# A streaming encoder step: softmax maps combined out of PSUM, group norms placed later, cache outputs placed in the last projection

## The chip, the core and the metric

The kernel runs on one core of one Trainium2 chip. The metric is device time in microseconds: the time of one execution, given as the median of the runs. Engines are called PE (TensorE), DVE (VectorE), ACT (ScalarE), POOL (GpSimd) and SP (SyncE, which here issues nearly all DMAs).

## What is computed

Two layers over 512 prompt tokens and 32 sample tokens, width 1024, all in float32. Layer 0 is RWKV-7 time mixing and is not touched. Layer 1, which the change edits, is differential attention with 12 heads of width 128, plus four memory heads, a SiLU gate, an output projection and a final norm:

```python
def diff_attention(q, k_all, v_all, q_pos, k_pos, lam):
    ...
    mask = k_pos[None, :] < (q_pos[:, None] // CHUNK + 1) * CHUNK
    def probs(qa, ka):
        s = jnp.einsum('bqhd,bkhd->bhqk', qa, ka).astype(jnp.float32) * DF_HD ** -0.5
        return jax.nn.softmax(jnp.where(mask, s, NEG_INF), axis=-1)
    attn = probs(q1, k1) - lam * probs(q2, k2)
    return jnp.einsum('bhqk,bkhd->bqhd', attn.astype(v_all.dtype), v_all)
...
    o = rmsnorm(o, subln) * (1.0 - lam_init)
    y_mem = mem_attention(qm, mk, mv)
    out = jnp.concatenate([o.reshape(B, T, MIX_W).astype(x.dtype), y_mem], axis=-1) * jax.nn.silu(gate)
    return x + out @ w_out, k, v
```

The keys and values of all heads are outputs too (the caches). The 32 sample tokens attend to 128 cached keys and to themselves. Since the result of each head is normed over its 128 values, a common factor per row can be applied late, if the norm's epsilon sees the scaled values.

## The kernel before, in words

Layer 1 is one long stream of projections (`stream`, line 1742). Each block of 128 output columns takes 48 matmul positions: two halves of 272 tokens, eight slices of the contraction, three products each (high and low parts of float32 numbers kept as `float32r`). The list `makes` in `diff_layer` (line 1777) holds 56 such blocks: values, keys and queries of each head, gates (`GATES1` says under which head), and query and gate of a memory head under the heads in `MEM1`. Everything else is a small step hung into this stream with `at(position, step)`. The position counts the matmuls since the stage's start, and `f` is the position at which the head's blocks begin. So the numbers at the top of the file (`TILES1`, `BACK1`, `SUMS1`, `NORM1`, `SAMPLE1`, `MEMAT1`, those with a 2 for the last heads) are distances in matmuls. While `self.ordered` is set, the wrapper `Queue` (line 111) ties each instruction of PE, DVE, ACT and SP to the one before it on its engine, so those four run in the order written; POOL isn't tied. Instructions issued after `self.ordered = False` are placed by the framework.

The steps of one head, in order:

- `values_turn`, `keys`, `keys_out`: DVE transposes of v and k, written by SP to a DRAM scratch `scr`, one pair per group of four heads (keys and values).
- `scores(t)` for four tiles of 128 queries (line 1872): PE makes two maps (`ps_s`, tag "c" of the pool `psc`, two banks), DVE masks them and takes the maxima (`peaks`, `snm`).
- `powers(t)`: ACT takes the exponentials of both maps into `pt` in SBUF, with row sums in `rs` (`srs` in the profile).
- `turned(t)`: DVE inverts both sums, multiplies the second with minus lambda, scales the second map (`TENSOR_SCALAR`) and adds the scaled first (`SCALAR_TENSOR_TENSOR`; `combine`, line 2107), then transposes 32x32 blocks into `pk`.
- `weights_out`, `weights_back`: SP writes `pk` to DRAM (`ptr`) and reads it back as `aT`, a full transposition, with the head's values `vt`.
- `weighted` (line 1923): PE multiplies `aT` and `vt` into `ps_o` (pool `psx`, one bank); DVE copies to `ot`, ACT sums squares into `ss`.

The last head transposes on PE instead (`turned_here`, `ps_aT`). Per group of four heads, the sample tokens have their own chain (`sample_scores` to `sample_rows`, tiles `ps_sc`, `ps_saT`, `ps_os`, `ps_osT`), and then `norms` (an inverse square root of nine small DVE instructions on `oss`), `scaled` (four DVE multiplications of `ot`) and `finished` (PE transposes into `ps_oT`, pool `psm`, two banks; DVE multiplies with the gate in `og`). `kv_out` (line 2029) copies a group's `scr` to the output caches: for groups 0 and 1 inside the stream, under the second head of the next group; for group 2 in the last projection, after the first half of its third output block.

The last projection (`w_out`, line 1238, with `consume` of `layer1`, line 1721) makes eight output blocks in two halves each, adds the residual and collects the squares of the final norm. The halves of the last block are followed at once by the final outputs.

Of the kernel before, what the change touches and what calls it, by code (L numbers as in the profile page):

```python
# [9 lines left out]
F32 = mybir.dt.float32  # L10
# [3 lines left out]
AF = mybir.ActivationFunctionType  # L14
# [30 lines left out]
BACK1, SUMS1, NORM1 = 96, 160, 182  # L45
BACK2, SUMS2, NORM2 = 50, 100, 40
SUMS3 = 22
OUT1 = 36
RKV = 4
# [72 lines left out]
class Trunk:  # L122
# [1538 lines left out]
    def layer1(self):  # L1661
# [17 lines left out]
        with ExitStack() as ctx:  # L1679
# [97 lines left out]
    def diff_layer(self, p, mp, mctx, pool_early, order, made):  # L1777
# [6 lines left out]
        def at(pos, fn):  # L1784
            ev.append((pos, len(ev), fn))

        def copied(x):
# [75 lines left out]

        def exps(S, nm):
            n = S[0].shape[1]
            rs = p.tile([P, 2], F32, tag="srs", name="srs", bufs=3)
            pt = p.tile([P, 2, 512], F32, tag="pt", name="pt", bufs=2)
            for m in range(2):
                self.ae.activation(pt[:, m, :n], S[m], AF.Exp, bias=nm[:, m : m + 1], accum_out=rs[:, m : m + 1])
            return pt, rs  # L1870

        def scores(st, t):
            n, c, S = (t + 1) * P, slice(t * P, t * P + P), []
            if t == 0:
                st["pk"] = pk = p.tile([P, 40, 32], F32, tag="pk", name="pk", bufs=PKB)
                st["aT"] = pk[:].rearrange("p (i b) c -> p i (b c)", b=4)
            for m in range(2):
                ps = self.psc.tile([P, 512], F32, tag="c", name="ps_s")
                for i, x in enumerate((st["kh"], self.kz[st["h"] % 2])):
# [5 lines left out]
        def powers(st, t):  # L1885
            st["pt", t] = exps(*st["pt", t])

        def mixed(pt, rs, n):
            self.ve.reciprocal(rs[:], rs[:])
            self.combine(pt, rs, n, nlam)  # L1890

        def joined(st, t):
            mixed(*st["pt", t], (t + 1) * P)

        def turned(st, t):
            n, b0 = (t + 1) * P, 2 * t * (t + 1)
            joined(st, t)
            pt, rs = st.pop(("pt", t))
            self.ve.transpose(st["pk"][:, b0 : b0 + 4 * (t + 1)].rearrange("p b c -> p (b c)"), pt[:, 0, :n])

        def turned_here(st, t):
            n, i0 = (t + 1) * P, t * (t + 1) // 2
            pt, rs = st.pop(("pt", t))
            ps = self.psm.tile([P, 512], F32, tag="m", name="ps_aT")
            for i in range(t + 1):
                self.te.transpose(ps[:, i * P : i * P + P], pt[:, 0, i * P : i * P + P], self.ident[:])
            self.ae.copy(st["aT"][:, i0 : i0 + t + 1, :], ps[:, :n].rearrange("p (i c) -> p i c", c=P))
# [15 lines left out]
        def weighted(st):  # L1923
# [11 lines left out]
            for t in range(4):  # L1935
                jk = p.tile([P, P], F32, tag="jk", name="jk", bufs=1)
                self.ae.activation(jk[:], ot[:, t, :], AF.Square, accum_out=G["ss"][:, 0, 4 * j + t : 4 * j + t + 1])

        def opened(G, hg):
            G["scr"] = [self.dp.tile([T, 4, P], F32, tag=f"scr{i}", name=f"scr{i}", bufs=2) for i in range(2)]  # L1940
            G["on"] = []
# [18 lines left out]
        def sample_scores(G):  # L1960
            ps = [self.psc.tile([P, 512], F32, tag="c", name="ps_sc") for _ in range(2)]
# [6 lines left out]
            G["sp"] = exps(*peaks([x[:, : P + TS] for x in ps]))  # L1968
            G["vs"] = vs = p.tile([P, 4, P], F32, tag="ck", name="vs")
            self.se.dma_start(vs[:TS], G["scr"][1][TP:])  # L1970

        def sample_mixed(G):
            mixed(*G["sp"], 160)

        def sample_turned(G):
            pt, rs = G.pop("sp")
            ps = self.psm.tile([P, 512], F32, tag="m", name="ps_saT")
            self.te.transpose(ps[:, :P], pt[:, 0, :P], self.ident[:])
            self.te.transpose(ps[:TS, P : 2 * P], pt[:, 0, P:160], self.ident[:])
            G["saT"] = aT = p.tile([P, 2 * P], F32, tag="aTs", name="aTs")  # L1980
# [3 lines left out]
        def sample_weighted(G):  # L1984
            aT = G["saT"]
            po = self.psx.tile([P, 512], F32, tag="x", name="ps_os")
            for j in range(4):
# [6 lines left out]
            G["os"] = os_ = p.tile([P, P], F32, tag="os", name="os")  # L1994
            G["s2"] = s2 = p.tile([P, 3], F32, tag="os2", name="os2")
            self.ve.tensor_copy(os_[:], po[:, :P])
            jk = p.tile([P, P], F32, tag="jk", name="jks", bufs=1)
            self.ae.activation(jk[:], os_[:], AF.Square, accum_out=s2[:, 0:1])

        def sample_norm(G):  # L2000
            os_, s2 = G["os"], G["s2"]
            self.ve.tensor_scalar(s2[:, 1:2], s2[:, 0:1], 1.0 / P, EPS, ALU.mult, ALU.add)
            self.rsqrt(s2[:, 2:3], s2[:, 1:2], p, "nt1")
            self.ve.tensor_scalar(os_[:], os_[:], s2[:, 2:3], None, ALU.mult)

        def sample_rows(G):
            psT = self.psx.tile([P, 512], F32, tag="x", name="ps_osT")
            self.te.transpose(psT[:, :P], G["os"][:], self.ident[:])
# [19 lines left out]

        def kv_out(G, hg, n):
            for i in range(2):  # L2030
                if n in (None, i):
                    self.se.dma_start(o[4 + i][0, 0, :, 4 * hg : 4 * hg + 4, :], G["scr"][i][:TP])
                    self.se.dma_start(o[10 + i][0, 0, :, 4 * hg : 4 * hg + 4, :], G["scr"][i][TP:])

# [4 lines left out]
        for h, st in enumerate(sts):  # L2039
# [12 lines left out]
            for t, (x, y) in enumerate(TILES2 if last else TILES1):  # L2052
# [50 lines left out]
        while ev:  # L2103
            ev.pop(0)[2]()
        return lambda: kv_out(groups[2], 2, None)

# [81 lines left out]
```

## Time and profile before

| what | value |
|---|---|
| median of 3 runs | 1410.56 us (1408.18 to 1410.85) |
| the profiled execution | 1410.36 us, its span 1408.6 us |
| busy in the span | PE 95%, PE weight loads 91%, DVE 65%, ACT 56%, POOL 41% |
| attention stage, about 806 to 1302 us of the span | 496 us, PE 470.7, DVE 308.3, ACT 241.6, POOL 202.1 |
| last projection and outputs, 1302 us to the end | 107 us, PE 97.4, DVE 46.2 |

Busy times are those of the span, so they are set against 1408.6 us. Matmuls are pipelined, and a busy PE may still run at half clock, which a separate column shows. An answer on waits names the waiting engine and its tile, then who released it last; a group of instructions has its count, its busy time and the mean of one. Nearly all instructions carry line 119, that of the wrapper, so tiles tell them apart.

### The profile page before, as it was taken

The page shows a single profiled execution, that of the slowest core. Times are in us where ns is not written, and L with a number is a line of the kernel's source. Part 1 is how long each engine was busy: PE and PEld are TensorE (multiplying, and loading weights), DVE is VectorE, ACT ScalarE, POOL GpSimd, SP SyncE. Part 2 cuts the span into 40 slices and gives each one's busy share as a digit, 9 for nine tenths or more (in the row PEclk, how much of TensorE's full clock was granted, in tenths as well). Part 3 has the DMA queues.
Part 4 walks back from the last instruction along what each step waited for, and adds up shares of the span by engine and source line. Part 5 has one row for each costly group of instructions (what it writes and reads, how often), then busy time and mean ns, then how long its engine had stood idle before and what let it go on. Part 6 is the DMA issues. An engine that isn't in the chain of part 4 may idle for free. (4 is left out here: it accounts for less than half of the span.)

```text
span 1408.6 us, 31401 instructions
## 1 busy us (share of the span) xinstructions
PE 1341.4 (95%) x11652; PEld 1281.3 (91%) x11652; DVE 921.3 (65%) x2210; ACT 787.4 (56%) x2189; POOL 571.6 (41%) x988
## 2 busy tenths in 40 slices
PE   6999999999999999899999999999989999997997
PEld 6998899999999998898899999999889998887997
DVE  7765777787778787665753556466664676657543
ACT  7665677777777777565533355454344554453421
POOL 2227577566756586520120064443333533443000
PEclk9999999999999999999999999999999999999999
DMA  7542222322233322333464476646475576582321
GB/s 238 174 138 70 64 57 78 84 75 70 71 84 84 73 64 78 93 90 101 140 180 128 135 187 166 148 109 151 137 176 129 137 174 167 122 213 76 106 68 64
DMA packets 387011, 165.46 MB, mean 117 GB/s; under 512 B 169561, under 2 KB 371298, under 8 KB 386858
## 3 DMA queue, kind: packets, MB, share of 16 engines
q1 hardware_dynamic: 386714, 162.92, 43.8%
q8 instruction: 92, 1.51, 0.5%
q10 hardware_dynamic: 144, 0.52, 0.1%
q14 instruction: 61, 0.50, 0.1%
HBM read 127.83 MB, written 38.90 MB: 118 GB/s over the span
## 5 line engine op out<-in xcount | busy, mean ns | idle before, releaser
L119 PE MATMUL ps_g<-hh,wlo 128*128 128x272 f32 x1808 | 538.0, 298 | 2.8 <-DVE wlo L119 1.5
L119 PE MATMUL ps_g<-hh,whi 128*128 128x272 f32 x1808 | 539.2, 298 | 1.3 <-ACT hh L119 0.9
L119 PE MATMUL ps_g<-hl,whi 128*128 128x272 f32 x1808 | 533.8, 295 | 0.6 <-POOL hl L491 0.5
L119 PEld LDWEIGHTS ps_g<-hh,wlo 128*128 128x128 f32 x1808 | 344.0, 190 | 7.1 <-DVE wlo L119 2.3
L119 PEld LDWEIGHTS ps_g<-hh,whi 128*128 128x128 f32 x1808 | 344.6, 191 | 5.7 <-ACT hh L119 1.3
L119 PEld LDWEIGHTS ps_g<-hl,whi 128*128 128x128 f32 x1808 | 344.1, 190 | 4.3 <-POOL hl L491 0.7
L119 ACT CAST whi<-raw 128x512 fp32r<-128x512 f32 x322 | 191.4, 618 | 99.7 <-PE ps_g L119 56.3
L329 POOL TENSOR_TENSOR wlo<-raw,whi 128x512 fp32r<-128x512 f32 x110 | 145.5, 1338 | 242.2 <-ACT whi L119 240.0
L780 POOL TENSOR_TENSOR tm<-u,m 102x84 f32<-102x84 f32 (+23 forms) x372 | 159.9, 430 | 167.3 <-DMA m<-sc 139.2
L119 DVE TENSOR_TENSOR wlo<-raw,whi 128x512 fp32r<-128x512 f32 x212 | 154.4, 743 | 68.5 <-ACT whi L119 66.9
L782 POOL TENSOR_TENSOR u<-u,tm 102x84 f32<-102x84 f32 (+23 forms) x372 | 158.9, 427 | 29.1
L119 PE MATMUL ps_g<-lo,whi 128*128 128x272 f32 x512 | 147.5, 289 | 0.7 <-DVE lo L119 0.7
L119 PE MATMUL ps_g<-hi,wlo 128*128 128x272 f32 x512 | 147.5, 289 | 0.0
L119 PE MATMUL ps_g<-hi,whi 128*128 128x272 f32 x512 | 146.5, 289 | 0.0
L119 PEld LDWEIGHTS ps_g<-lo,whi 128*128 128x128 f32 x512 | 96.4, 188 | 1.1 <-DVE lo L119 1.1
L119 PEld LDWEIGHTS ps_g<-hi,wlo 128*128 128x128 f32 x512 | 96.5, 189 | 0.2 <-DVE wlo L119 0.2
L119 PEld LDWEIGHTS ps_g<-hi,whi 128*128 128x128 f32 x512 | 96.3, 189 | 0.0
L119 ACT ACTIVATE pt<-ps_s,snm 128x128 f32<-128x128 f32 (+3 forms) x96 | 49.7, 524 | 58.5 <-DVE snm L119 58.5
L119 DVE SCALAR_TENSOR_TENSOR SB<-ps_c,dl,sd 64x64 f32<-64x64 f32 x168 | 47.4, 282 | 44.3 <-PE ps_c L119 39.2
L119 ACT COPY sv<-ps_c 64x64 f32<-64x64 f32 x192 | 39.2, 204 | 37.8 <-PE ps_c L119 36.0
L119 DVE SCALAR_TENSOR_TENSOR qp<-ps_g,qp 64x272 fp32r<-64x272 f32 x48 | 21.1, 439 | 46.9 <-ACT qp L119 46.6
L1631 POOL TENSOR_TENSOR hl<-hn,hh 128x544 fp32r<-128x544 f32 x8 | 12.2, 1533 | 93.4 <-ACT hh L119 93.3
(373 smaller groups left out, 2560.9 us busy)
## 6 DMA issues: line engine op xcount, KB each, us to landing
raw<-in_rw_in_dram SPq DMA_DIRECT2D x114, 256.0 KB
raw<-in_df_in_dram SPq DMA_DIRECT2D x112, 256.0 KB
raw<-in_w_out_dram SPq DMA_DIRECT2D x64, 256.0 KB
ptr<-pk SPq DMA_DIRECT2D x44, 160.0 KB
aT<-ptr SPq DMA_DIRECT2D x11, 640.0 KB
scr<-sg SPq DMA_DIRECT2D x96, 68.0 KB
out_dram<-scr SPq DMA_DIRECT2D x6, 1024.0 KB
m<-sc SPq DMA_DIRECT2D x36, 128.0 KB
```

The costliest lines, as they stand in the source:

```text
L119: return lambda *a, **k: self.trunk.tie(self, issue(*a, **k))
L329: todo.append((lambda k=k, q=q: low.tensor_tensor(lo[:, k], raw[q][:], hi[:, k].bitcast(F32), ALU.subtract), LATER))
L780: nc.gpsimd.tensor_tensor(tm[:, :n, :wd], u3[:, :n, kx : kx + 1].to_broadcast(sh), m3[:, kx : kx + 1, kx + 1 :].to_broadcast(sh), ALU.mult)
L782: nc.gpsimd.tensor_tensor(u3[:, :n, kx + 1 :], u3[:, :n, kx + 1 :], tm[:, :n, :wd], ALU.add)
L1631: nc.gpsimd.tensor_tensor(self.hl[:, k, :], h[:], self.hh[:, k, :].bitcast(F32), ALU.subtract)
```

## The change

- `scores` takes the bank of map 0 from `psx` and that of map 1 from `psc`. `exps` writes the first exponentials to SBUF and the second back into their own PSUM bank; in the last head (and the last group's sample tokens) the second go to an SBUF tile `pm`.
- `mixed` no longer scales the first map. It makes the factor s0 * (minus lambda) / s1 and adds the second map with that factor to the first, in one `scalar_tensor_tensor`. The sums s0 are kept per group, inverted once per head, and enter the squares (as ACT's scale) and the norms (one more small multiplication).
- `ps_o`, `ps_os` and `ps_osT` move from `psx` to `psm`. `pk` has two buffers, `scr` three.
- Positions: tiles, samples, reads and sums as in the constants; the norms of groups 0 and 1 are placed from the start of the head after next, 30 positions in, and their `scaled` and `finished` steps lie 14 and 24 positions apart (8 and 16 before).
- The gate of head 7 is made under head 8, the fourth memory head under head 7.
- All six `kv_out` copies (two DMAs each) are written in the last projection, one after the second half of each output block from the third on.

```diff
-QB, KB, PKB = 2, 1, 1
+QB, KB, PKB = 2, 1, 2
-GATES1 = {h: (h,) for h in range(8)}
+GATES1 = {**{h: (h,) for h in range(7)}, 8: (7,)}
-MEM1 = (1, 3, 5, 8)
-TILES1 = ((156, 174), (186, 204), (216, 234), (246, 266))
+MEM1 = (1, 3, 5, 7)
+TILES1 = ((156,178),(188,210),(220,244),(254,280))
-SAMPLE1 = ((280, "s"), (308, "m"), (328, "t"), (346, "w"), (362, "n"), (392, "r"))
-SAMPLE2 = ((196, "s"), (222, "m"), (236, "t"), (256, "w"), (311, "n"), (336, "r"))
-TILES2 = ((156, 188), (216, 242), (244, 274), (276, 308))
-BACK1, SUMS1, NORM1 = 96, 160, 182
-BACK2, SUMS2, NORM2 = 50, 100, 40
+SAMPLE1 = ((310, "s"), (338, "m"), (362, "t"), (386, "w"), (402, "n"), (430, "r"))
+SAMPLE2 = ((186, "s"), (214, "m"), (228, "t"), (248, "w"), (311, "n"), (336, "r"))
+TILES2 = ((152, 180), (210, 236), (240, 268), (272, 304))
+BACK1, SUMS1, NORM1 = 88, 160, 30
+BACK2, SUMS2, NORM2 = 56, 104, 40
-OUT1 = 36
+OUT1 = 24
...
-                if k == 2 and not v.start:
-                    kv_out()
+                if k >= 2 and v.start and kv_out:
+                    kv_out.pop(0)()
...
-        def exps(S, nm):
-            n = S[0].shape[1]
+        def exps(S, nm, s0, here):
             rs = p.tile([P, 2], F32, tag="srs", name="srs", bufs=3)
-            pt = p.tile([P, 2, 512], F32, tag="pt", name="pt", bufs=2)
-            for m in range(2):
-                self.ae.activation(pt[:, m, :n], S[m], AF.Exp, bias=nm[:, m : m + 1], accum_out=rs[:, m : m + 1])
-            return pt, rs
+            pt = p.tile([P, 512], F32, tag="pt", name="pt", bufs=2)[:, : S[0].shape[1]]
+            self.ae.activation(pt, S[0], AF.Exp, bias=nm[:, 0:1], accum_out=s0)
+            pm = S[1] if here else p.tile([P, 512], F32, tag="pm", name="pm", bufs=1)[:, : S[1].shape[1]]
+            self.ae.activation(pm, S[1], AF.Exp, bias=nm[:, 1:2], accum_out=rs[:, 0:1])
+            return pt, pm, rs, s0
+
+        def bank(m, name):
+            pool, tag = ((self.psx, "x"), (self.psc, "c"))[m]
+            return pool.tile([P, 512], F32, tag=tag, name=name)
...
-        def mixed(pt, rs, n):
-            self.ve.reciprocal(rs[:], rs[:])
-            self.combine(pt, rs, n, nlam)
+            c = 4 * st["j"] + t
+            st["pt", t] = exps(*st["pt", t], st["G"]["s0"][:, c : c + 1], st["h"] < DH - 1)
+
+        def mixed(pt, pm, rs, s0):
+            self.ve.reciprocal(rs[:, 0:1], rs[:, 0:1])
+            self.ve.scalar_tensor_tensor(rs[:, 1:2], rs[:, 0:1], nlam, s0, ALU.mult, ALU.mult)
+            self.ve.scalar_tensor_tensor(pt, pm, rs[:, 1:2], pt, ALU.mult, ALU.add)
 
         def joined(st, t):
-            mixed(*st["pt", t], (t + 1) * P)
+            mixed(*st["pt", t])
+            if t == 3:
+                s0 = st["G"]["s0"][:, 4 * st["j"] : 4 * st["j"] + 4]
+                self.ve.reciprocal(s0, s0)
...
-            po = self.psx.tile([P, 4, P], F32, tag="x", name="ps_o")
+            po = self.psm.tile([P, 4, P], F32, tag="m", name="ps_o")
...
-                self.ae.activation(jk[:], ot[:, t, :], AF.Square, accum_out=G["ss"][:, 0, 4 * j + t : 4 * j + t + 1])
+                c = slice(4 * j + t, 4 * j + t + 1)
+                self.ae.activation(jk[:], ot[:, t, :], AF.Square, scale=G["s0"][:, c], accum_out=G["ss"][:, 0, c])
...
             self.rsqrt(ss[:, 2, :], ss[:, 1, :], p, "nt16")
+            self.ve.tensor_tensor(ss[:, 2, :], ss[:, 2, :], G["s0"][:], ALU.mult)
...
-                at(f + y + norm, lambda G=G: norms(G))
+                b, s, r = (f + y + NORM2, 8, 14) if last else (begin(h + 2) + NORM1, 14, 24)
+                at(b, lambda G=G: norms(G))
                 for j in range(4):
-                    at(f + y + norm + 18 + 8 * j, lambda G=G, j=j: scaled(G, j))
-                    at(f + y + norm + (30 + 10 * j if last else 56 + 16 * j), lambda G=G, hg=hg, j=j: finished(G, hg, j))
-            if hg and h % 4 == 1:
-                for n in range(2):
-                    at(f + 24 + 96 * n, lambda G=groups[hg - 1], hg=hg, n=n: kv_out(G, hg - 1, n))
+                    at(b + 18 + s * j, lambda G=G, j=j: scaled(G, j))
+                    at(b + 30 + r * j, lambda G=G, hg=hg, j=j: finished(G, hg, j))
```

More of the change, by code (lines that the diff above doesn't have):

```diff
@@ L1785, in at, with begin @@
             ev.append((pos, len(ev), fn))
+        def begin(h):
+            return 6 * KT * sum(3 + len(GATES1.get(x, ())) + 2 * (x in MEM1) for x in range(h))
         def copied(x):
@@ L1874, in scores @@
             if t == 0:
+                if st["j"] == 0:
+                    st["G"]["s0"] = p.tile([P, 16], F32, tag="os0", name="os0", bufs=2)
                 st["pk"] = pk = p.tile([P, 40, 32], F32, tag="pk", name="pk", bufs=PKB)
@@ L1877, in scores @@
             for m in range(2):
-                ps = self.psc.tile([P, 512], F32, tag="c", name="ps_s")
+                ps = bank(m, "ps_s")
                 for i, x in enumerate((st["kh"], self.kz[st["h"] % 2])):
@@ L1936, in weighted @@
                 jk = p.tile([P, P], F32, tag="jk", name="jk", bufs=1)
-                self.ae.activation(jk[:], ot[:, t, :], AF.Square, accum_out=G["ss"][:, 0, 4 * j + t : 4 * j + t + 1])
+                c = slice(4 * j + t, 4 * j + t + 1)
+                self.ae.activation(jk[:], ot[:, t, :], AF.Square, scale=G["s0"][:, c], accum_out=G["ss"][:, 0, c])
         def opened(G, hg):
-            G["scr"] = [self.dp.tile([T, 4, P], F32, tag=f"scr{i}", name=f"scr{i}", bufs=2) for i in range(2)]
+            G["scr"] = [self.dp.tile([T, 4, P], F32, tag=f"scr{i}", name=f"scr{i}", bufs=3) for i in range(2)]
             G["on"] = []
@@ L1960, in sample_scores @@
         def sample_scores(G):
-            ps = [self.psc.tile([P, 512], F32, tag="c", name="ps_sc") for _ in range(2)]
+            ps = [bank(m, "ps_sc") for m in range(2)]
             for c, ks in ((slice(0, P), G["ckT"]), (slice(P, P + TS), G["ks"])):
@@ L1967, in sample_scores @@
                                        tile_position=(64 * m, 32 * j))
-            G["sp"] = exps(*peaks([x[:, : P + TS] for x in ps]))
+            G["s2"] = s2 = p.tile([P, 4], F32, tag="os2", name="os2")
+            G["sp"] = exps(*peaks([x[:, : P + TS] for x in ps]), s2[:, 3:4], G is not groups[-1])
             G["vs"] = vs = p.tile([P, 4, P], F32, tag="ck", name="vs")
@@ L1972, in sample_mixed @@
         def sample_mixed(G):
-            mixed(*G["sp"], 160)
+            mixed(*G["sp"])
+            self.ve.reciprocal(G["s2"][:, 3:4], G["s2"][:, 3:4])
         def sample_turned(G):
-            pt, rs = G.pop("sp")
+            pt = G.pop("sp")[0]
             ps = self.psm.tile([P, 512], F32, tag="m", name="ps_saT")
-            self.te.transpose(ps[:, :P], pt[:, 0, :P], self.ident[:])
-            self.te.transpose(ps[:TS, P : 2 * P], pt[:, 0, P:160], self.ident[:])
+            self.te.transpose(ps[:, :P], pt[:, :P], self.ident[:])
+            self.te.transpose(ps[:TS, P : 2 * P], pt[:, P:], self.ident[:])
             G["saT"] = aT = p.tile([P, 2 * P], F32, tag="aTs", name="aTs")
@@ L1985, in sample_weighted @@
             aT = G["saT"]
-            po = self.psx.tile([P, 512], F32, tag="x", name="ps_os")
+            po = self.psm.tile([P, 512], F32, tag="m", name="ps_os")
             for j in range(4):
@@ L1994, in sample_weighted @@
             G["os"] = os_ = p.tile([P, P], F32, tag="os", name="os")
-            G["s2"] = s2 = p.tile([P, 3], F32, tag="os2", name="os2")
             self.ve.tensor_copy(os_[:], po[:, :P])
             jk = p.tile([P, P], F32, tag="jk", name="jks", bufs=1)
-            self.ae.activation(jk[:], os_[:], AF.Square, accum_out=s2[:, 0:1])
+            self.ae.activation(jk[:], os_[:], AF.Square, scale=G["s2"][:, 3:4], accum_out=G["s2"][:, 0:1])
         def sample_norm(G):
@@ L2003, in sample_norm @@
             self.rsqrt(s2[:, 2:3], s2[:, 1:2], p, "nt1")
-            self.ve.tensor_scalar(os_[:], os_[:], s2[:, 2:3], None, ALU.mult)
+            self.ve.tensor_scalar(os_[:], os_[:], s2[:, 2:3], s2[:, 3:4], ALU.mult, ALU.mult)
         def sample_rows(G):
-            psT = self.psx.tile([P, 512], F32, tag="x", name="ps_osT")
+            psT = self.psm.tile([P, 512], F32, tag="m", name="ps_osT")
             self.te.transpose(psT[:, :P], G["os"][:], self.ident[:])
@@ L2027, in finished, with kv_out @@
             self.ve.tensor_tensor(g[:, TP:], G["oT"][:, 32 * j : 32 * j + 32], g[:, TP:], ALU.mult)
[L2029 to L2033, printed above, removed]
+        def kv_out(hg, i):
+            scr = groups[hg]["scr"][i]
+            self.se.dma_start(o[4 + i][0, 0, :, 4 * hg : 4 * hg + 4, :], scr[:TP])
+            self.se.dma_start(o[10 + i][0, 0, :, 4 * hg : 4 * hg + 4, :], scr[TP:])
         groups = [{} for _ in range(3)]
@@ L2057, in diff_layer @@
                     at(f + y + 12, lambda st=st, t=t: turned_here(st, t))
-            back, sums, norm = (BACK2, SUMS2, NORM2) if h >= DH - 2 else (BACK1, SUMS1, NORM1)
+            back, sums = (BACK2, SUMS2) if h >= DH - 2 else (BACK1, SUMS1)
             for off, fn in ((124, values_back),) if last else ((y + (8 if h == DH - 2 else OUT1), weights_out), (y + back, weights_back)):
@@ L2104, in diff_layer @@
             ev.pop(0)[2]()
-        return lambda: kv_out(groups[2], 2, None)
+        return [lambda hg=hg, i=i: kv_out(hg, i) for hg in range(3) for i in range(2)]
     def combine(self, pt, rs, n, nlam):
```

10 lines of the change are left out of this document (4 added, 6 removed).

## The prediction

> **What bounds the kernel now.** I read the page first, then the busy times and granted clock of single stretches, then what TensorE (PE) waits for in each stretch, then the groups of one stretch by shape, and last the queue of SyncE (SP).
>
> ```profile
> span 1408.6 us, 31401 instructions
> PE 1341.4 (95%) x11652; PEld 1281.3 (91%) x11652; DVE 921.3 (65%) x2210; ACT 787.4 (56%) x2189; POOL 571.6 (41%) x988
> 806.00:1302.00 496.00, 470.69 (x3675) 455.16 (x3674) 308.32 (x738) 241.62 (x717) 202.06 (x153) 0.98 0.61 150
> ```
>
> The last row is the attention stage, the only one the change edits besides the last projection: after the duration, busy us of PE, PE's weight loads, VectorE (DVE), ScalarE (ACT) and GpSimd (POOL), then clock, DMA share, GB/s. PE is the bound, but it is not gapless. Its waits, over 806–1000, 1000–1020, 1020–1060, 1135–1150, 1150–1190, 1190–1235 and, from the fourth line from the end, 1235–1302 (columns: us in total, times, longest):
>
> ```profile
> PE ps_saT L119 <- DVE mrs L119: 0.9, 1, 0.9
> PE ps_s L119 <- ACT pt L119: 2.8, 2, 1.7
> PE ps_oT L119 <- DVE ot L119: 0.5, 1, 0.5
> PE ps_o L119 <- DMA aT<-ptr: 4.4, 1, 4.4
> PE ps_saT L119 <- DVE pt L119: 2.3, 1, 2.3
> PE ps_oT L119 <- DVE og L119: 2.9, 1, 2.9
> PE ps_s L119 <- ACT pt L119: 1.9, 2, 1.3
> PE ps_oT L119 <- DVE ot L119: 4.8, 2, 4.3
> PE ps_aT L119 <- DVE ps_s L119: 1.4, 1, 1.4
> PE ps_aT L119 <- DVE os L119: 1.1, 1, 1.1
> PE ps_o L119 <- DMA aT<-ptr: 0.4, 1, 0.4
> ```
>
> All but the two aT waits come back to DVE being late, directly or through ACT. After five of these waits PE also runs at half clock (column 0.50):
>
> ```profile
> 1047.10:1053.90 6.80, 4.49 (x21) 4.52 (x22) 0.00 (x0) 0.94 (x4) 0.86 (x1) 0.50 0.66 193
> 1146.10:1149.50 3.40, 3.40 (x17) 3.40 (x16) 1.27 (x3) 1.54 (x5) 0.59 (x1) 0.50 0.94 139
> 1183.60:1187.00 3.40, 3.40 (x18) 3.40 (x17) 1.88 (x4) 2.01 (x5) 0.95 (x1) 0.50 0.36 108
> ...
> 1296.20:1303.00 6.80, 4.81 (x21) 4.44 (x22) 5.75 (x11) 0.37 (x1) 0.30 (x1) 0.50 0.00 0
> ```
>
> Work done at half clock costs half its time again: 4.49/2 = 2.2 us, then 1.7 us for each stretch of 3.40.
>
> **The change part by part.** Positions in the code count matmuls of the main stream, 0.126 us each (42.30 us for 336, in the chain below).
>
> *Combining out of PSUM.* The second exponentials stay in their bank, the first are never scaled, and one DVE instruction with a PSUM operand replaces a scaling plus a combining.
>
> ```profile
> L119 DVE SCALAR_TENSOR_TENSOR pt<-pt,srs 128x256 f32<-128x256 f32 x12 | 14.9, 1243 | 0.4
> L119 DVE SCALAR_TENSOR_TENSOR pt<-pt,srs 128x512 f32<-128x512 f32 x12 | 14.5, 1209 | 0.4
> L119 DVE SCALAR_TENSOR_TENSOR pt<-pt,srs 128x384 f32<-128x384 f32 x12 | 10.6, 885 | 0.4
> L119 DVE SCALAR_TENSOR_TENSOR pt<-pt,srs 128x128 f32<-128x128 f32 x12 | 4.2, 351 | 0.4
> L119 DVE TENSOR_SCALAR pt<-pt,srs 128x512 f32<-128x512 f32 x12 | 7.9, 661 | 0.4
> ...
> L119 DVE TENSOR_SCALAR pt<-pt,srs 128x256 f32<-128x256 f32 x12 | 6.1, 511 | 0.4
> ...
> L119 DVE TENSOR_SCALAR pt<-pt,srs 128x384 f32<-128x384 f32 x12 | 5.1, 421 | 0.4
> ...
> L119 DVE TENSOR_SCALAR pt<-pt,srs 128x128 f32<-128x128 f32 x12 | 3.4, 287 | 0.4
> L119 DVE SCALAR_TENSOR_TENSOR og<-og,ps_mo 128x512 f32<-128x512 f32 x4 | 2.7, 687 | 5.1 <-PE ps_mo L119 5.1
> L119 DVE SCALAR_TENSOR_TENSOR og<-og,ps_g 128x272 f32<-128x272 f32 x32 | 13.9, 434 | 31.2 <-ACT og L119 31.0
> L119 DVE COPY os<-ps_os 128x128 f32<-128x128 f32 x3 | 0.9, 292 | 2.7 <-PE ps_os L119 2.7
> L119 DVE RECIPROCAL srs<-srs 128x2 f32<-128x2 f32 x51 | 8.2, 160 | 14.9 <-ACT pt L119 14.6
> ```
>
> Combining costs 44.2 us and scaling 22.5, together 66.7. The SBUF-only form is slower at width 256 than at 512, so something other than its own work stretches it; the same operation with one PSUM operand runs with its width (434 ns at 272, 687 at 512). Taking 0.29, 0.42, 0.55 and 0.69 us for the four widths, eleven heads cost 21.5 us; the last head keeps SBUF and its 44.2/12 = 3.7. That frees 41.5 us of DVE. Back come 15 reciprocals of 0.16 and three small multiplications in the norms (0.16, up to about 1.2 if stretched): 3 to 6 us. DVE goes from 308 to about 271 us, some 3 us less per head. ACT writing PSUM is in no row; its count of exponentials is unchanged. I take no change: the same operation waits 63.5 us for DVE in the stage (row below), so a tenth of a microsecond either way is covered; uncovered, 44 of them would be 4 us, either way.
>
> [...]
>
> *Second pk buffer.* A DVE that waits for the DMA out of pk holds all maxima queued behind it; two buffers remove these waits:
>
> ```profile
> ACT pt L119 <- DVE snm L119: 63.5, 32, 4.5
> DVE pk L119 <- DMA ptr<-pk: 6.2, 4, 1.8
> ```
>
> *PSUM banks.* Scores use psx for map 0 and two psc buffers for map 1. Map 0 still waits only for the previous first exponential, as now. Map 1's bank is held until the combination, 22 to 26 positions (about 3 us) after the scores; the next tile takes the other buffer and the one after that starts 64 positions later, so no wait. The weighted sums (ps_o) and two sample tiles go to psm, two buffers shared with all transposes. Apart from the last head, neighbours lie mostly 10 or more positions apart. In head 11, ps_o of head 10, a transpose and the sample's sum lie within 8 positions (about 1 us), and the DVE copy that frees ps_o takes about 0.7: I charge 1.0 us, bounds 0 and 2.
>
> *Cache copies.* Four pairs leave the stage's ordered queue. One stood right ahead of the values and weights of head 4:
>
> ```profile
> 1036.96 2.03 SPq L119 DMA_DIRECT2D out_dram<-scr  x2
> 1039.09 1.08 SPq L119 DMA_DIRECT2D raw<-in_df_in_dram  x2
> 1040.21 0.74 SPq L119 DMA_DIRECT2D vt<-scr  x1
> 1041.45 0.70 SPq L119 DMA_DIRECT2D aT<-ptr  x1
> ...
> 1260.93 3.08 SPq L119 DMA_DIRECT2D out_dram<-scr  x4
> 1302.55 42.30 PE ps_g L119 x336
> ```
>
> This is the place of the 4.4 us wait; without 2.03 us of issue and the transfer itself, and with 72 positions instead of 64 between read and use, I count it gone with its half clock. Will the copies really lie under the last projection? Those of group 2 are written there in the code already (third output block, 216 matmuls after 1302.55, so near 1330), yet were issued at 1260.93: outside the hand-ordered stretch the framework places them as soon as it can. I expect all twelve transfers early, in gaps of SP's queue. Behind the burst of 1260.93 PE has no wait for a DMA (the 0.4 is for an aT issued ahead of it): zero. If they do stay late, the last pair goes out just ahead of the final outputs: 0 to 3 us (2 of issue, the rest sharing); I take 0.
>
> *Moved steps.* The sample's steps come 30 to 40 positions later and are spread wider, with their vs load on SP; the norms start 62 positions later for group 0 and 14 for group 1, with transposes 24 apart instead of 16; memory head 3 moves from head 8 to head 7, with its loads, away from group 1's transposes. All this is the same PE work. Each head's tail comes 14 positions later and overlaps the next head; head 11 starts its tail 4 earlier (0.5 us, ignored).
>
> *The sum.* Gone: 0.9 + 2.8 + 0.5 + 4.4 + 2.3 + 2.9 + 1.9 = 15.7 us of waits, and 2.2 + 1.7 + 1.7 of half clock (the third follows the 2.9 wait, and is like the second): 21.3. Half of 1.4 + 1.1 in head 11: 1.2. The tail, 4.8 and its half clock, stays. Given back: the norms still meet tiles 2 and 3 of the following head, a quarter of 0.5 + 2.8 + 2.9, 1.5; psm 1.0; one half-clock stretch at a new place, 1.7. Net 18.3 us. The profiled run took 1410.36 (span 1408.6 plus 1.8), 0.2 under the median: 1410.4 − 18.3 = **1392.1**.
>
> On the clock, the trace shows 3.40 us at 0.50 after a wait of only 2.3. [...]
>
> **Rivals.**
> 1. *psm becomes the queue* (slower). Eighteen uses (12 ps_o, 6 sample tiles) join a pool whose banks DVE and ACT free; DVE was up to 4.3 us late. At 1.0 us a use the gain is spent; at 1.5 it is 27 us, 1419. For: close neighbours around the samples of heads 3, 7 and 11. Against: DVE is lighter and steps are spread.
> 2. *The copies do not do what the title says and hit a weights read*: dispatched in the attention stage, a burst delays one aT as at 1041. 4.4 + 2.2 come back: 1398.7. For: 1260.93. Against: that burst hit none.
> 3. *The relief does not reach PE*: norms and tiles collide as before, or DVE is freed of 20 us rather than 41. Half of the DVE-caused waits (11.3) and both 1.7 stay: 1392.1 + 5.6 + 3.4 = 1401.
> 4. *Given back in full* elsewhere: 1410.
>
> **How the numbers follow.** Forecast 0.53, rival 2 0.16, rival 3 0.17, rival 4 0.04, rival 1 0.10. Low end: nothing given back (−4.2) and most of the tail's waits shrink too (some 7 us): 1381. High end: rivals 2 and 3 together, 1408, which leaves out about 0.14 above. Time 1392. Faster 0.86, same 0.04, slower 0.10, where same means within 0.2%, about 3 us, the least a measurement of this kernel can tell.
>
> **What would show it.** Right: combining groups near 0.4–0.7 us with a PSUM source; no pk wait for ptr; no wait of ps_o for aT; DVE near 271 us; half-clock stretches three fewer. Copies issued before the last projection settle their place. Wrong: PE waits of ps_o or ps_mm for a bank (rival 1); a wait for aT (rival 2); ps_oT and ps_s waits as before (rival 3); a PSUM-fed combination over 1 us; the span ending on copies.

## The result and the profile after

The changed kernel takes 1384.34 us (median of 4 runs, 1383.9 to 1385.31) against 1409.37 us for the kernel before on the same chip (4 runs, 1407.05 to 1410.85): ratio 0.9825, 95% interval 0.9808 to 0.9842, or 25 us less. The forecast was 1392.1 and 18.3 less, with a range of 1381 to 1408; the time lies inside it, near its low end. Run again beside the experiments, it took 1382.71 us (5 runs) against 1410.63: ratio 0.9806 [0.9784, 0.9827].

The first lines of the page of the changed kernel, and then two stretches of it (columns as in the prediction: duration, busy time of PE, its weight loads, DVE, ACT, POOL, then clock, DMA share, GB/s): the attention stage, which now ends at 1276, and the only part of it at half clock.

```profile
span 1382.1 us, 31367 instructions
PE 1330.9 (96%) x11652; PEld 1274.6 (92%) x11652; DVE 885.9 (64%) x2177; ACT 794.1 (57%) x2189; POOL 565.9 (41%) x988
```

```profile
806.00:1276.00 470.00, 461.77 (x3686) 449.67 (x3684) 273.72 (x711) 249.67 (x721) 198.12 (x153) 0.99 0.65 159
1269.60:1276.40 6.80, 4.50 (x21) 4.41 (x22) 6.12 (x12) 1.14 (x2) 0.77 (x1) 0.50 0.01 2
```

PE is idle for 470.00 − 461.77 = 8.2 us of the stage, where it was 496.00 − 470.69 = 25.3. DVE is down to 273.7 us (forecast 271). Of five half-clock stretches one is left, in the tail. This is the whole list of PE's waits in the changed kernel's stage (us in total, times, longest); the same list of the kernel before adds up to 25.1 us, this one to 8.0:

```profile
PE ps_oT L119 <- DVE ot L119: 4.7, 2, 4.5
PE ps_aT L119 <- DVE pt L119: 2.1, 2, 1.5
PE ps_osT L119 <- DVE og L119: 1.0, 1, 1.0
PE ps_o L119 <- DMA aT<-ptr: 0.2, 1, 0.2
```

The combining of the changed kernel, by shape (count, then busy us and mean ns):

```profile
L119 DVE SCALAR_TENSOR_TENSOR pt<-ps_s,srs,pt 128x512 f32<-128x512 f32 x11 | 8.3, 751 | 0.4
L119 DVE SCALAR_TENSOR_TENSOR pt<-ps_s,srs,pt 128x384 f32<-128x384 f32 x11 | 6.8, 618 | 0.4
L119 DVE SCALAR_TENSOR_TENSOR pt<-ps_s,srs,pt 128x256 f32<-128x256 f32 x11 | 5.3, 485 | 0.4
L119 DVE SCALAR_TENSOR_TENSOR pt<-ps_s,srs,pt 128x128 f32<-128x128 f32 x11 | 3.9, 351 | 0.4
L119 DVE SCALAR_TENSOR_TENSOR pt<-pm,srs,pt 128x512 f32<-128x512 f32 x1 | 1.7, 1718 | 0.0
```

They run with their width: 24.3 us in eleven heads (forecast 21.5). The last head, still out of SBUF, takes 1.7 us for one tile of 512.

And SP's queue of the changed kernel at the three bursts of copies, and at the read that was late before (start, time that issuing took):

```profile
964.47 3.73 SPq L119 DMA_DIRECT2D out_dram<-scr  x4
1035.35 0.37 SPq L119 DMA_DIRECT2D aT<-ptr  x1
1120.74 2.51 SPq L119 DMA_DIRECT2D out_dram<-scr  x4
1237.19 3.05 SPq L119 DMA_DIRECT2D out_dram<-scr  x4
```

All twelve copies go out in the attention stage. None lies under the last projection, though they are written there.

**A measure that layer 0 doesn't disturb.** Layer 0, which is the same in both kernels, has its third half-clock stretch at 265.4 us in the kernel before and at 402.6 in the changed one, and over the fourteen traces the stage begins between 807.40 and 811.08 us. So beside the times I use the stage alone, in each kernel's profiled run: from the last `ps_r` of layer 0 to the first 336 products of the last projection. In the kernel before, from its timeline:

```profile
807.78 0.30 PE L119 MATMUL ps_r<-dg,ones 128*128 128x32 f32 x2
```

With the chain's row at 1302.55 (in the prediction) that is 494.8 us. In the changed kernel, timeline and chain:

```profile
809.22 0.30 PE L119 MATMUL ps_r<-dg,ones 128*128 128x32 f32 x2
```

```profile
1276.23 42.14 PE ps_g L119 x336
```

467.0 us, 27.8 less; in its second profile it was 466.5. The last projection and outputs kept their length (1408.6 − 1302.55 = 106.1 and 1382.1 − 1276.23 = 105.9).

| kernel | time, us | ratio [95%] | stage, us | PE waits in it, us |
|---|---|---|---|---|
| before | 1409 to 1414 | 1 | 494.8 | 25.1 |
| changed | 1384.34 | 0.9825 [0.9808, 0.9842] | 467.0 | 8.0 |
| changed, again | 1382.71 | 0.9806 [0.9784, 0.9827] | 466.5 | 7.9 |
| before + combining alone | 1402.16 | 0.992 [0.9899, 0.9942] | 483.5 | 19.4 |
| before + copies alone | 1406.49 | 0.9946 [0.9927, 0.9965] | 490.4 | 22.6 |
| before + positions alone | 1397.94 | 0.99 [0.9871, 0.993] | 482.0 | 20.9 |
| changed, copies back | 1385.6 | 0.9799 [0.978, 0.9818] | 470.8 | 11.9 |
| changed, norms back | 1384.58 | 0.9792 [0.9773, 0.981] | 467.5 | 9.0 |
| changed, one pk | 1384.02 | 0.9813 [0.9792, 0.9834] | 467.9 | 9.1 |
| changed, one pk, combining from SBUF | 1387.59 | 0.984 [0.9819, 0.9861] | 472.2 | 12.3 |
| changed, memory head back | 1386.16 | 0.983 [0.9806, 0.9854] | 470.0 | 11.0 |
| changed, copies held | 1382.62 | 0.9793 [0.9773, 0.9814] | 466.3 | 7.9 |
| changed, last root in PSUM | 1381.27 | 0.9785 [0.9763, 0.9807] | 463.8 | 5.9 |
| the same, last head from PSUM too | 1379.61 | 0.9769 [0.9748, 0.979] | 461.9 | 4.7 |

### The profile page after: what moved, and what is told of

Same layout as the page of the kernel before. It is cut to its first block, busy times and chain, and to the rows that moved or that the text cites. A ratio compares the mean times of both kernels' runs of the same rounds, so it can differ in the third digit from the quotient of the medians.

```text
span 1382.1 us, 31367 instructions
## 1 busy us (share of the span) xinstructions
PE 1330.9 (96%) x11652; PEld 1274.6 (92%) x11652; DVE 885.9 (64%) x2177; ACT 794.1 (57%) x2189; POOL 565.9 (41%) x988
## 5 line engine op out<-in xcount | busy, mean ns | idle before, releaser
L329 POOL TENSOR_TENSOR wlo<-raw,whi 128x512 fp32r<-128x512 f32 x110 | 142.1, 1309 | 198.2 <-ACT whi L119 197.5
L1849 POOL TENSOR_TENSOR kz<-k,kh 64x544 fp32r<-64x544 f32 x24 | 33.2, 1384 | 51.9 <-ACT kh L119 51.0
L1631 POOL TENSOR_TENSOR hl<-hn,hh 128x544 fp32r<-128x544 f32 x8 | 12.4, 1563 | 93.1 <-ACT hh L119 93.1
```

The lines of the kernel that those rows point to most:

```text
L329: todo.append((lambda k=k, q=q: low.tensor_tensor(lo[:, k], raw[q][:], hi[:, k].bitcast(F32), ALU.subtract), LATER))
L1631: nc.gpsimd.tensor_tensor(self.hl[:, k, :], h[:], self.hh[:, k, :].bitcast(F32), ALU.subtract)
L1849: nc.gpsimd.tensor_tensor(self.kz[h % 2][rows[m], m, :], k[rows[m], :], hi.bitcast(F32), ALU.subtract)
```

## The experiments

The theory was the prediction's: DVE was late, the copies held up one read, and with both mended PE's waits and their half clock go. The rivals were that one part does it all, or that a part does nothing, and that the PSUM operand as such brings little.

**Parts alone, on the kernel before**

*The softmax edit* (banks, second exponentials in PSUM, no scaling; positions, one pk and copies as before):

```diff
-            self.combine(pt, rs, n, nlam)
+            self.ve.scalar_tensor_tensor(rs[:, 1:2], rs[:, 0:1], nlam, s0, ALU.mult, ALU.mult)
+            self.ve.scalar_tensor_tensor(pt, pm, rs[:, 1:2], pt, ALU.mult, ALU.add)
```

> The kernel before with the softmax edit alone (second exponentials in PSUM, first unscaled, ps_o and the sample tiles in psm); positions, pk, memory head 3 and cache copies as before. Theory (DVE's lateness makes most of PE's waits): DVE loses some 35 us in the attention stage, two thirds of the 11.3 us of DVE-caused waits and the 3.4 us of half clock behind them go, the 4.4 us wait for aT with its 2.2 stays: 8 to 12 us faster, 1397 to 1401. Rival (the new positions do it, DVE was only badly ordered): DVE loses the same 35 us but the waits stay, 1407 to 1410.

Measured: 12.0 us less (1414.19 to 1402.16), the stage 11.3. Three rows of its waits:

```profile
PE ps_o L119 <- DMA aT<-ptr: 5.6, 3, 2.9
PE ps_s L119 <- ACT pt L119: 3.0, 4, 1.1
PE ps_oT L119 <- DVE og L119: 3.0, 1, 3.0
```

Both waits of ps_saT are gone. The late reads of aT stay (5.6 us, three times), and so does the 2.9 us wait of the transposes, now 3.0. Of the 11.3 us of waits for DVE ahead of the last head, 6.3 are left: less than half went, not the two thirds expected. Idle time is 5.9 of the 11.3 us that the stage became shorter; 3.8 are half clock, for PE does 11.8 us of its work at half clock here, against 19.4. Of these 3.8, 2.2 are the stretch behind head 4's read, which still made PE wait 2.9 us: here the wait fell across two windows of the clock (last section), which is luck. The lighter DVE brought 11 to 12 us by itself in this run, luck included, and it is not the whole.

*The copies* (written in the last projection, `scr` with three buffers; all else as before):

```diff
-            if hg and h % 4 == 1:
-                for n in range(2):
-                    at(f + 24 + 96 * n, lambda G=groups[hg - 1], hg=hg, n=n: kv_out(G, hg - 1, n))
```

> The kernel before with the cache copies alone written in the last projection (and three scr buffers). Theory: the copies are issued early all the same, about 20 us after each group's last keys; the 4.4 us wait for aT in head 4 and its 2.2 us of half clock go, all DVE-caused waits stay: 1402 to 1404. Rival (the copies were harmless, aT was late for DVE's sake): within 1.5 us of 1409.

Measured: 7.7 us less (1414.19 to 1406.49), of which the profile shows 4.4 in the stage. The wait of head 4 for aT is gone, but not through the copies alone. Counted from the start of the stage, the read went out 2.0 us earlier; PE came for it 1.6 us later, after a half-clock stretch at 1021.3 that the kernel before doesn't have; and the read took at least 0.8 us less from issue to use. Then another one for aT comes up, in head 10 at 1254, where the kernel before had 0.4:

```profile
PE ps_o L119 <- DMA aT<-ptr: 2.7, 1, 2.7
```

The read it waits for was issued at 1250.19, ahead of the third burst of copies (1256.02), so the burst didn't delay its issue. In the kernel before the same read went out at 1255.08 and PE came for it at 1260.73; here PE comes at 1254.61, 6.1 us earlier for a read only 4.9 earlier: a stall taken away uncovers the next. The read also took 1.1 us longer from issue to use (7.1 against 6.0); whether the burst, issued while it was under way, had a part in that, this run doesn't show.

*The positions* (the constants of the diff and the place of the norms; softmax, pk and copies as before):

```diff
-TILES1 = ((156, 174), (186, 204), (216, 234), (246, 266))
+TILES1 = ((156,178),(188,210),(220,244),(254,280))
-MEM1 = (1, 3, 5, 8)
+MEM1 = (1, 3, 5, 7)
```

> The kernel before with the new positions alone (tiles, samples, reads, sums, norms later, the gate of head 7 and the fourth memory head moved); scaling and combining stay in SBUF, the copies stay in the stage, one pk. Theory (the load on DVE is what decides, and the copies): the positions alone remove collisions only in part, waits of ps_s, ps_saT and ps_oT for DVE remain at 4 to 9 us, the aT wait of head 4 goes or shrinks because its read has 72 positions instead of 64; gain 3 to 9 us, about 1402 to 1407. Rival (the three parts give the same waits, each removes them by itself): 15 us or more, below 1395. A time not better than before (0 to -2 us) would mean that the positions do nothing without the lighter DVE.

Measured: 13.6 us less (1411.56 to 1397.94), the stage 12.8. That is more than the 3 to 9 I expected and less than the rival's 15. The first four rows of its waits up to 1283 us, ahead of the tail's 4.6:

```profile
PE ps_o L119 <- DMA aT<-ptr: 5.1, 2, 2.9
PE ps_oT L119 <- DVE ot L119: 2.4, 2, 1.2
PE ps_sc L119 <- ACT pt L119: 1.9, 1, 1.9
PE ps_s L119 <- ACT pt L119: 1.8, 2, 0.9
```

Waits for aT remain, the one of head 4 with 2.9 us of its 4.4: a third less with 72 positions instead of 64. But combining alone, with 64, had 2.9 there as well, so the positions aren't shown to be the reason, nor is it shown that the copies hold the rest. With DVE hardly lighter (303.3 us busy in the stage, 306.5 before), its waits ahead of the last head shrink from 11.3 to 5.2 us (in the last head one of 1.9 is new), and no half-clock stretch is left in the stage except the tail's. Idle time is only 4.3 of the 12.8 us; 7.2 are half clock, again in part by luck, since the windows of head 4's wait are idle for 1.8 and 1.2 us. In time, spreading the steps brought as much as making DVE faster; in waits, each brought 4 to 6 us. The stages of the three parts save 11.3 + 4.4 + 12.8 = 28.5 us, the whole change 27.8 and 28.3: they nearly add up, but by chance. The waits by themselves fall short (5.7 + 2.5 + 4.2 = 12.4 of 17.1), since what one part leaves late is not the same place in each. The half clock is counted more than once: PE's work at half clock falls from 19.4 us to 11.8, 15.2 and 5.1 in the three, some 13 us of time in sum, and to 4.5 in the whole change, 7.4 us of time. The second pk buffer is in none of the three.

**Parts undone, on the changed kernel**

*The copies back in the stage:*

```diff
+            if hg and h % 4 == 1:
+                for n in range(2):
+                    at(f + 24 + 96 * n, lambda G=groups[hg - 1], hg=hg, n=n: kv_out(G, hg - 1, n))
```

> The changed kernel with only the cache copies back at their old places. Theory: ps_o of head 4 waits again for aT, 3 to 4.5 us, with a half-clock stretch behind it: 4 to 7 us slower, 1388 to 1391. Rival (72 positions between read and use and a pk that is free earlier absorb the copy): 1384 to 1386.

The time is that of the change by its ratio (0.9799), and 1385.6 us lies where the rival had it; but the stage is 3.8 to 4.3 us longer. The waits for aT are back, and SP's queue shows how: two copies stand ahead of the reads of head 4, and the aT read is 2.10 us in issue, where it took 0.37.

```profile
PE ps_o L119 <- DMA aT<-ptr: 3.9, 3, 1.8
```

```profile
1031.32 2.23 SPq L119 DMA_DIRECT2D out_dram<-scr  x2
...
1036.81 2.10 SPq L119 DMA_DIRECT2D aT<-ptr  x1
```

No half clock follows these waits, and the tail here got one window of half clock instead of two, which hides part of it in the time. So the theory holds for the waits in the stage, not for the half clock, and the loss doesn't show in the time.

*The norms at their old distance:*

```diff
-                b, s, r = (f + y + NORM2, 8, 14) if last else (begin(h + 2) + NORM1, 14, 24)
+                norm = NORM2 if last else NORM1
+                at(f + y + norm, lambda G=G: norms(G))
```

> The changed kernel with only the norms, scalings and transposes of groups 0 and 1 at their old distances (182 after the last tile, 8 and 16 apart). Theory (the lighter DVE carries them anywhere): 0 to 3 us slower, 1384 to 1387. Rival (the placing is what removed the waits of ps_oT and ps_s): 6 to 8 us slower with at least one half-clock stretch, 1390 to 1392.

1384.58 us, the stage 467.5, one small wait of ps_s more (1.0 us in all). The tail here got one window of half clock instead of two (3.1 us of work in it instead of 4.5), which hides some 0.7 us. So placing the norms later, which the title names, is worth between 0.5 and 1.7 us once DVE is light.

*The changed kernel again, one pk buffer, and combining from SBUF.* The last has one pk too, so it is read against the second.

```diff
-QB, KB, PKB = 2, 1, 2
+QB, KB, PKB = 2, 1, 1
```

```diff
-            pm = S[1] if here else p.tile([P, 512], F32, tag="pm", name="pm", bufs=1)[:, : S[1].shape[1]]
+            pm = p.tile([P, 512], F32, tag="pm", name="pm", bufs=2)[:, : S[1].shape[1]]
```

> The changed kernel itself, as the yardstick of this group: 1.75 per cent under the kernel before, as in the first measurement (ratio 0.9825).

> The changed kernel with one pk buffer. Theory: DVE waits some 4 to 6 us again for the DMA out of pk, with maxima queued behind it, but PE has slack now: 0 to 2 us slower than the changed kernel. Rival (the second buffer carries a good part of the gain): a ps_s wait of 1 to 3 us and a half-clock stretch come back, 3 to 5 us slower.

> As the kernel with one pk buffer, but the second exponentials of all heads go to SBUF (two pm buffers), so the one combining instruction has two SBUF inputs. Same instructions, same positions; read against the kernel with one pk. Theory (an SBUF-only combination is held up by GpSimd's SBUF traffic): the 256- to 512-wide combinations rise from 0.49 to 0.75 us to 0.9 to 1.3 us, DVE gets 15 to 20 us busier, PE waits of 2 to 4 us come back: 3 to 6 us slower. Rival (dropping the scaling was the relief, the operand's place doesn't matter): combinations keep their times, within 1.5 us.

One pk costs 1.3 us (1382.71 to 1384.02; stage 1.4): DVE waits 2.7 us for ptr again, PE 1.0 for ps_s. From SBUF it costs another 3.6 us (stage 4.3), with new waits of ps_oT and ps_s of 0.4 to 0.9 each. So the time came as the theory said, but DVE's load did not. Two rows of the combining from SBUF:

```profile
L119 DVE SCALAR_TENSOR_TENSOR pt<-pm,srs,pt 128x384 f32<-128x384 f32 x12 | 11.8, 980 | 0.4
L119 DVE SCALAR_TENSOR_TENSOR pt<-pm,srs,pt 128x256 f32<-128x256 f32 x12 | 5.8, 485 | 0.4
```

At 384 and 512 (832 ns) it is stretched, at 256 not at all: 485 ns, exactly what the PSUM form takes, where the kernel before had 1243. All of it is 31.8 us, only 4.3 more than the 27.5 out of PSUM. The traces show when it happens, instruction by instruction. In the kernel before, 20 of the 51 combinations (samples included) start while POOL is in the middle of a `TENSOR_TENSOR`; these 20 are stretched, by 0.9 to 1.1 us, and no other is. Here three start so and two 0.02 us ahead of one, and these five are stretched; twelve into which a POOL instruction starts only later are not. In the changed kernel two PSUM-fed ones start while POOL runs, and keep their time. So it takes both, two SBUF operands and that moment; without the scaling in front of it the combination mostly starts ahead of such an instruction or clear of it.

*The fourth memory head and the gate back under their old heads:*

```diff
-GATES1 = {**{h: (h,) for h in range(7)}, 8: (7,)}
-MEM1 = (1, 3, 5, 7)
+GATES1 = {h: (h,) for h in range(8)}
+MEM1 = (1, 3, 5, 8)
```

> The changed kernel with memory head 3 back under head 8 and the gate of head 7 under head 7, all else as changed. Theory: group 1's norms meet the memory head's steps again; the lighter DVE carries most of it, 0 to 2 us slower. Rival (moving the memory head removed the 2.9 us wait of ps_oT): that wait of 2 to 3 us with its 1.7 us of half clock comes back, 4 to 5 us slower.

3.5 us slower (1386.16; stage 3.5 longer than in the repeat), between the two expectations, and for another reason than either gave: a wait for the read of aT in head 7, and 0.8 us more of ps_oT.

```profile
PE ps_o L119 <- DMA aT<-ptr: 2.3, 2, 2.1
```

The read is not later: it goes out 335.1 us after the start of the stage, 335.2 in the repeat. PE comes for it sooner, 5.5 us after its issue; in the repeat 9.9 us pass, and there is no wait. In between PE has 37 products of the stream instead of 53, and the memory head's transposes and products (2.8 us) no longer stand there. So the move of the memory head, which I had only taken as clearing group 1's transposes, also gives that read time.

**The tail, and where the copies lie**

*The last group's inverse root in PSUM.* In the tail of the changed kernel the small norm instructions of DVE (16 values per partition), and beside them POOL's four subtractions:

```profile
1265.19 1.34 DVE L119 TENSOR_TENSOR nt<-nt,oss 128x16 f32<-128x16 f32 x1
1266.56 1.27 DVE L119 SCALAR_TENSOR_TENSOR oss<-nt,oss 128x16 f32<-128x16 f32 x1
1267.87 1.25 DVE L119 TENSOR_TENSOR nt<-oss 128x16 f32<-128x16 f32 x1
1269.15 1.25 DVE L119 TENSOR_TENSOR nt<-nt,oss 128x16 f32<-128x16 f32 x1
1270.43 0.17 DVE L119 SCALAR_TENSOR_TENSOR nt<-nt 128x16 f32<-128x16 f32 x1
```

```profile
1265.02 5.35 POOL L1684 TENSOR_TENSOR lo<-og,hi 128x544 fp32r<-128x544 f32 x4 [9.56 <-ACT hi L119]
```

Four of them take 1.25 to 1.34 us each, the step of POOL's (5.35/4); as soon as POOL ends at 1270.37 they take 0.17. The edit keeps the running value in a PSUM bank, so that each reads at most one operand from SBUF:

```diff
+        ps = self.psx.tile([P, 512], F32, tag="x", name="ps_r16")
+        y, u = ps[:, :16], ps[:, 16:32]
...
-            self.rsqrt(ss[:, 2, :], ss[:, 1, :], p, "nt16")
+            if G is groups[-1]:
+                G["r"] = self.root(x, G["s0"], p)
+                return
```

> The change, with the inverse root of the last group's norms kept in PSUM, so that each of its small DVE instructions reads at most one SBUF operand. Nothing is left out. Theory (these instructions take 1.25 to 1.35 us each because they wait in step with POOL's reads of SBUF, and the last transpose waits for them): they run at 0.1 to 0.3 us each beside POOL, the wait of ps_oT in the tail falls from 4.5 us to under 1.5, and its half-clock stretch shrinks from 6.8 to 3.4 or goes; 4 to 6 us faster than the change, 1377 to 1380. Rival 1 (POOL slows any DVE instruction alike, or what is late is ACT or the sums): the instructions stay near 1.3 us, time unchanged within 1 us. Rival 2: the wait goes but another of the tail's chain (ps_aT, aT, the gates) ends last: 0 to 2 us faster.

```profile
1264.63 0.16 DVE L119 TENSOR_TENSOR nt<-nt,ps_r 128x16 f32<-128x16 f32 x1
1264.71 1.27 DVE L119 TENSOR_TENSOR og<-osT,og 128x32 f32<-128x32 f32 x1
1265.90 0.17 DVE L119 SCALAR_TENSOR_TENSOR ps_r<-nt,ps_r 128x16 f32<-128x16 f32 x1
1266.11 0.17 DVE L119 TENSOR_TENSOR nt<-oss,ps_r 128x16 f32<-128x16 f32 x1
1266.31 0.18 DVE L119 TENSOR_TENSOR ps_r<-nt,ps_r 128x16 f32<-128x16 f32 x1
```

POOL is busy here just the same (5.32 us from 1264.53). The instructions with a PSUM operand take 0.17 us; the one between them with two SBUF operands takes 1.27. So what is held up beside POOL here is the instruction with two SBUF operands, not those with one. The long wait of ps_oT falls from 4.5 to 1.0 us, the half clock from two windows to one. The time, 1381.27 us, falls less than the 4 to 6 us expected: the stage by 2.7 to 3.2, because 1.0 of ps_oT waiting for a bank and 0.5 of ps_o come up instead, and one window of half clock stays.

*The last head out of PSUM as well:*

```diff
-            st["pt", t] = exps(*st["pt", t], st["G"]["s0"][:, c : c + 1], st["h"] < DH - 1)
+            st["pt", t] = exps(*st["pt", t], st["G"]["s0"][:, c : c + 1], True)
```

> As the run with the root in PSUM, and the last head too combines out of PSUM instead of out of the SBUF tile. Nothing is left out. Theory (the 512-wide combination of the last head takes 1.72 us for the same reason, two SBUF operands beside POOL, and the transposes ps_aT wait for it): it falls to about 0.75 us, the waits of ps_aT from 2.2 to under 1 us, 1 to 2 us faster than the run with the root alone. Rival (the banks held by the second map delay the next scores in the last head, whose tiles are closest together): a new wait of ps_s of 1 to 3 us, no gain or slower by up to 2 us.

```profile
1252.26 0.75 DVE L119 SCALAR_TENSOR_TENSOR pt<-ps_s,srs,pt 128x512 f32<-128x512 f32 x1
```

From 1.72 to 0.75 us, while POOL runs as before (2.52 us from 1250.92); the waits of ps_aT fall from 2.2 to 1.3, and no wait of ps_s appears. The stage is 1.9 us shorter again, with no half clock left in it: 1379.61 us, 0.9769 of before. The intervals of this and the change overlap ([0.9748, 0.979] and [0.9784, 0.9827]); the waits and the stage, 461.9 against 466.5, say that it is the faster.

*The copies held back*, each tied behind the latest load of the projection's weights:

```diff
-            self.se.dma_start(raw[:], src[q * h * P : (q + 1) * h * P, c0 : c0 + P].rearrange("(k p) c -> p k c", p=P))
+            self.latest = self.se.dma_start(raw[:], src[q * h * P : (q + 1) * h * P, c0 : c0 + P].rearrange("(k p) c -> p k c", p=P))
...
+                self.order(self.se.dma_start(o[a + i][0, 0, :, 4 * hg : 4 * hg + 4, :], scr[b]), self.latest)
```

> The change, with each cache copy tied on SP behind the latest load of the projection's weights, so that all twelve really lie under the last projection. Theory (early or late, the copies meet nothing that PE waits for): within 1 us of the change, waits and half-clock stretches as there; at worst 3 us slower if the last pair goes out just ahead of the final outputs. Rival (the early bursts do cost, through the shared DMA engines and SP's queue, the remaining waits of the stage): the waits of ps_aT or ps_osT shrink and it is 1 to 3 us faster.

```profile
1305.42 1.24 SPq L119 DMA_DIRECT2D out_dram<-scr  x2
...
1317.97 2.32 SPq L119 DMA_DIRECT2D out_dram<-scr  x2
...
1331.82 1.19 SPq L119 DMA_DIRECT2D out_dram<-scr  x2
...
1337.86 5.07 SPq L119 DMA_DIRECT2D out_dram<-scr  x6
```

Now they do lie under the last projection, and it is the same time (1382.62 and 1382.71), stage and waits. So what the copies cost comes with their place in the ordered queue, ahead of a read; early in its gaps or late, they are free here.

## Why the prediction was right, and where its size was off

The direction and the mechanism held; the gain was 26.5 us in the profiled run (1410.36 to 1383.9), not 18.3. By the steps of the sum:

- *Waits gone, 15.7:* none of them is in the list of after, but for 0.2 of ps_oT at group 1's transposes. Right.
- *Half of head 11's ps_aT, 1.2:* measured 0.4. The lighter DVE doesn't reach the last head, whose 512-wide combination still took 1.72 us; 2.1 of 2.5 stayed, until that head too combined out of PSUM (1.3).
- *The tail's 4.8 stays:* right (4.5 of the 4.7 are there), and its half clock (4.50/2 = 2.25 us, before 2.4). That it comes back to DVE being late was only half of it: DVE was late because its small instructions were held up beside POOL, and with one operand in PSUM the wait fell to 1.0.
- *psm, given back 1.0:* it is the wait of ps_osT for a bank that DVE's og frees, 1.0, but at the first group's sample tokens (996.9 us), where DVE multiplies a memory head's output out of that bank, not in head 11. Rival 1 got its one wait.
- *Norms meeting tiles, given back 1.5:* nothing but the 0.2 named above. This step failed: a light DVE takes the norms nearly anywhere (norms back: one wait of 1.0).
- *Half clock, 5.6 gone and 1.7 given back:* four stretches went and none came. The fourth, at 1255.3, wasn't in my sum: PE is busy in it for 3.29 us, so 1.6. With 0.15 of the tail that is 2.2 + 1.7 + 1.7 + 1.6 + 0.15 = 7.4 instead of 3.9.
- *Not in the sum:* short waits of ps_g for `wlo` and `whi` (the low and high parts of the weights), 1.3 and 0.4 us before, are gone, and 0.3 elsewhere.

Waits: 15.7 + 0.4 + 1.7 + 0.3 − 1.0 = 17.1, which is 25.1 − 8.0. With the half clock 24.5. The stage became 27.8 shorter, and it began 1.4 us later (809.22 and 807.78). Some 3 us of the 27.8 lie in PE's busy time beside the half clock (it fell by 10.6 us, from 469.5 to 458.9); no run splits them. That the time came near the low end of the range is luck: that end had most of the tail's waits go, and they stayed, while the fourth stretch and these 3 us were not in the sum at all.

The attribution failed further than the sum. I gave nearly all waits behind DVE to its 40 us less work. The positions alone, with no work taken off DVE, did as much (12.8 and 11.3 us of stage, of which 4.2 and 5.7 are waits and most of the rest half clock, partly luck), and of the 11.3 us of waits for DVE ahead of the last head 5.2 and 6.3 were left: a wait for DVE says that DVE was late there, not that it had too much to do. And what the PSUM operand takes off DVE depends on the moment: the PSUM form is 27.5 us at the old positions (combining alone) and at the new ones, the SBUF form 44.2 in the kernel before, 40.6 with the new positions alone and 31.8 in the changed kernel with one pk, where no scaling runs ahead of it. The sure part of the relief is the scaling that is gone, 22.5 us. In the changed kernel the operand is worth 4.3 us of DVE and 3.6 of time. It was the nearest row, at 434 ns for 272, that sized the new form: 0.29, 0.42, 0.55 and 0.69 us forecast, 0.35, 0.49, 0.62 and 0.75 measured.

A combination out of PSUM is no dearer in itself: the rows give 485 and 351 ns from PSUM at 256 and 128, and 485 and 352 from SBUF undisturbed, and the sum charged nothing extra. The two half-clock stretches of 3.40 us behind the waits of 2.3 and 2.9 us went with their waits, as the sum counted them.

Rival 2 named the right object (a read of aT) and, with the copies held, the early bursts turned out free. Rival 3 is refuted for the whole change by the list of its waits; for the lighter DVE alone it came true, with 6.3 us of the 11.3 left. ACT got dearer by 7 us in the stage (241.0 to 248.0), more than half of it the 48 squares, 402 ns with a scale per row against 311; PE has no wait for ACT left, as assumed.

## What to carry to other kernels

Cost an edit's waits by where the late engine stands in its own order, not only by its load: respreading the steps and lightening the engine each brought some 12 us here, 4 to 6 of them in waits and most of the rest in half clock, and only the whole change took away nearly all waits for DVE ahead of the last head. Where a small DVE instruction takes 1.3 us, look at what POOL does in that moment; one operand in PSUM was the cure (0.17 us). Transfers that nobody waits for cost nothing here, early or late (1382.71 us, and 1382.62 with the copies held), but can make a read late when they stand just ahead of it in an ordered queue (3.9 us of waits with the copies back).

## What the hardware showed unexpectedly

**Half clock goes by windows.** In each trace all half-clock stretches begin at whole multiples of 3.413 us from each other, which is the length of a single stretch: 1047.1, 1146.1, 1183.6 and 1296.2 lie 29, 11 and 33 of them apart (249.1 us for the 73). Not every wait is followed by one. Two waits of 2.9 us, one in the kernel before and one with the combining alone, cut at the windows of their own trace:

```profile
1180.20:1183.60 3.40, 0.90 (x8) 0.90 (x9) 3.04 (x6) 1.29 (x5) 0.64 (x1) 1.00 0.80 138
```

```profile
1041.20:1044.60 3.40, 2.44 (x20) 2.23 (x18) 1.01 (x4) 2.04 (x6) 1.27 (x1) 1.00 1.09 301
1044.60:1048.00 3.40, 1.48 (x13) 1.51 (x14) 0.00 (x0) 0.00 (x0) 0.00 (x0) 1.00 0.98 268
1048.00:1051.40 3.40, 3.40 (x27) 3.22 (x27) 2.27 (x6) 1.55 (x7) 0.00 (x0) 1.00 0.09 23
```

The first falls into one window, which is idle for 2.5 us, and the next (1183.6) is at half clock. The second is shared by two, 1.0 and 1.9, and the clock stays at 1.00. Over the attention stages of all fourteen traces, of the windows at full clock, those idle for 1.95 us or more were followed by half clock 19 times of 19, those idle 1.6 to 1.95 us twice of 10, those of 1.0 to 1.6 once of 35, and none of 1842 below. The bound is not sharp: 1.90 was not followed, 1.62 once was. With the copies alone, the stretch at 1146 is gone though its wait of 2.3 us is still there, and a new one, at 1021.3, follows waits that are no longer than before. So the price of a 2 to 3 us wait is partly chance: the tail of one and the same kind has one window of half clock or two (copies held 3.4 us, repeat 6.8), and a forecast of such stretches at new places can only be a share, not a count.

**ACT writes PSUM a little faster than SBUF.** In the changed kernel the same exponential took 649 ns into its own bank and 686 into SBUF at 512 wide, 334 and 365 at 128.
